# Gated linear attention with all chunks scored against each other, and RWKV's projections of a half taken for both groups in the order k, r, v

## The chip, the cores and the metric

The kernel runs on one core of one Trainium2 chip. The metric is the device time of one execution in microseconds (us), the median of the runs; lower is better.

## The reference

x is (1, 256, 1024) in float32. A first block (a recurrent layer, a gated feed-forward layer, an attention layer, another feed-forward layer) is followed by a second block of two layers. Each of these two layers projects the normed input and runs three branches on it, a latent attention, an RWKV-7 recurrence and a gated linear attention (GLA), whose gated sum goes through one more projection. The change touches the last two branches. GLA has 4 heads with keys of 128 and values of 256, and the 256 frames are taken as 4 chunks of 64:

```python
cum = jnp.cumsum(log_a.reshape(b, nc, CHUNK, GLA_HEADS, GLA_DK), axis=2)
cum_last = cum[:, :, -1:]
q_dec = q * jnp.exp(cum)
k_inv = k * jnp.exp(-cum)
k_to_end = k * jnp.exp(cum_last - cum)
attn = jnp.einsum('bnihd,bnjhd->bnhij', q_dec, k_inv)
attn = jnp.where(jnp.tril(jnp.ones((CHUNK, CHUNK), bool)), attn, 0.0)
o_intra = jnp.einsum('bnhij,bnjhv->bnihv', attn, v)

def step(state, inp):
    q_c, k_c, v_c, d_c = inp
    o_c = jnp.einsum('bihd,bhdv->bihv', q_c, state)
    state = state * d_c[..., None] + jnp.einsum('bjhd,bjhv->bhdv', k_c, v_c)
    return state, o_c
```

RWKV has 16 heads of 64. Of its streams r, k and v, each shifted by one frame and mixed, the part that matters here is the norm of each head of k and the sum over r, k and r_k:

```python
kk = heads(k * k_k)
kk = kk / jnp.maximum(jnp.sqrt(jnp.sum(kk * kk, axis=-1, keepdims=True)), 1e-12)
k = k * (1 + (a - 1) * k_a)
...
bonus = jnp.sum(r_h * k_h * r_k.astype(f32), axis=-1, keepdims=True) * v_h
```

## The kernel before

All activations stay on the chip; what is streamed from memory is the weights. Every projection goes through `linear` (L303, output with features on the partitions) or `linear_tm` (L328, output with frames on the partitions). Both take a weight block with `weights` (L287): SP starts a DMA into one of four `raw` buffers, ACT casts it to a rounded upper part `hi` (L284), DVE subtracts to get the lower part `lo` (L285), and each product is three matmuls on the PE, hi by hi, hi by lo and lo by hi (L322 to L324 with 256 columns, L350 to L352 with 512). Small products that aren't projections are plain fp32 matmuls; the profile counts each of those twice (an instruction x4 shows as x8).

The program is written out as one stream, and a list scheduler, which counts with modelled times, sets the order of the instructions on each engine before the run. On the chip each engine takes its own list strictly in order and waits at semaphores. The PE's list is mostly projections, with the small products of the three branches put in between them.

The second block's layer `second` (L1022) runs, for each layer, the latent attention, RWKV in two halves (`rwkv`, L1453, hf = 0 and 1, 8 heads each) and GLA (`gla`, L1287). What follows a half of RWKV (inverse and chain) is given out in steps between the projections of the other branches.

One half of RWKV has two groups (g = 0 and 1, four heads each). For each group `rwkv_tiles` (L1478) does in turn: the two low-rank products for decay and gate (`pw`, `pa`, L1506 and L1507), their tanh and exponentials on ACT (L1511 to L1528) with a scan on DVE (L1516), the projection k, squares of k (`rkk`, L1536), the sums of squares over each head by a product with 2 columns (L1541), the root on POOL (`rsqrt`, `root`, L370 to L374, into `rri`), a copy on ACT that spreads it over each head (`rrw`, L1545), four 128x128 products that turn it (L1551), DVE's work on k, the projection r, DVE's products of r and k (L1566), 2-column products for the bonus (L1571), and the projection v. Then `rwkv_products` (L1575) makes the 16 score products of the group (L1585). So each half runs k0, r0, v0, products 0, k1, r1, v1, products 1.

GLA takes two heads at a time (q = 0 and 1). Decays relative to each chunk's own start sit in `ep` (for q), `en` (for k) and `et` (k to the end of its chunk), each 128x2x256. Per head: two transposes of `et` (L1369) and an ACT copy (`ket`), two 128x128 score products (L1375), a mask (`gat`, L1377) that keeps only the two 64x64 blocks on the diagonal, and then a chain over the four chunks: scores by v (L1391, 64x64; L1385 for the second pair of chunks at once), decayed q by the state (L1393), and the next state's addition (`pS`, L1396), which DVE or ACT makes into the state `gS`. One step's L1393 needs the state of the step before.

## Time and profile before

| | before |
|---|---|
| runs, us | 1886.73, 1888.77, 1895.27 (median 1888.77) |
| profiled execution, us | 1890.57, of which the span of the profile is 1888.8 |
| PE busy | 1817.2 us, 96% of the span |
| PE weight loads busy | 1517.8 us, 80% |
| DVE, ACT, POOL busy | 1287.9, 1037.9 and 114.9 us |
| mean granted clock of TensorE | 0.977 of full speed |
| read from memory | 291.58 MB, 156 GB/s over the span |

The profile is of one execution. Its own time, 1890.57 us, is 1.8 us above its span. "Busy" of the PE counts the modelled length of each matmul, and two neighbours overlap in it, so that the time from one start to the next is shorter than the length shown. An idle time stands in square brackets behind the instruction that came after it, with the engine and line whose end released it. The granted clock is a share of full speed: 1.00 is the level of 2.4 GHz and 0.50 that of 1.2 GHz.

### The profile page before, as it was taken

To read this page: it belongs to the slowest core of one execution; us is meant where nothing else is said; L and a number is where in the kernel's file an instruction comes from. 1 tells how busy PE (TensorE), PEld (TensorE's weight loads), DVE (VectorE), ACT (ScalarE), POOL (GpSimd) and SP (SyncE) were. 2 spreads that over 40 slices of the span, in tenths; PEclk is the share of its full clock that TensorE was granted. 3 is DMA by queue.
4 is the path that set the end of the run, shared out by engine and by line. 5 is a ranking of instruction groups with operands and counts; after the bars stand their busy time and mean duration, and the time that the engine had idled before them with its cause. 6 is when DMAs were issued, how large, how long until landed. Compare 5 with 4: busy or idle time off the path is not lost.

```text
span 1888.8 us, 31680 instructions
## 1 busy us (share of the span) xinstructions
PE 1817.2 (96%) x11984; PEld 1517.8 (80%) x11984; DVE 1287.9 (68%) x2824; ACT 1037.9 (55%) x2137; POOL 114.9 (6%) x255
## 2 busy tenths in 40 slices
PE   7999999999989998999999899997999999899997
PEld 6988778877668886998789877796998789877796
DVE  6988788757658874777557754575778566754575
ACT  6786645446544444765566544454665566534453
POOL 0000000002000000020001000100020001000100
PEclk9999999999999999999999899998999999899999
DMA  5534687755247775455244443354455334444263
GB/s 204 179 102 138 219 268 245 239 180 166 91 137 269 260 226 171 144 165 158 90 129 135 134 123 112 102 184 145 135 163 160 99 118 146 127 120 123 90 182 109
DMA packets 108873, 296.79 MB, mean 157 GB/s; under 512 B 34832, under 2 KB 36240, under 8 KB 108592
## 3 DMA queue, kind: packets, MB, share of 16 engines
q1 hardware_dynamic: 106496, 291.54, 48.9%
q10 hardware_dynamic: 2224, 3.22, 0.6%
q8 instruction: 94, 1.54, 0.3%
q14 instruction: 59, 0.48, 0.1%
HBM read 291.58 MB, written 3.15 MB: 156 GB/s over the span
## 4 chain that ended last, share of the span: by engine, by line
PE 53%; DVE 2%; DMA 2%; ACT 2%; POOL 1%; issue 0%; SPq 0%; DVEq 0%; POOLq 0%; ACTq 0%
PE pm L350 7%; PE pm L352 7%; PE pm L351 7%; PE pm L322 6%; PE pm L324 6%; PE pm L323 6%; PE pk L1585 2%; DMA dz<-rZ 1%; PE pS L1396 1%; PE ps L1257 1%; PE ps L1256 1%; DMA Gm<-dz 1%; PE po L1393 1%; PE pk L1692 1%; PE pk L1717 1%; PE po L1391 1%
## 5 line engine op out<-in xcount | busy, mean ns | idle before, releaser
L285 DVE TENSOR_TENSOR lo<-raw,hi 128x512 fp32r<-128x512 f32 (+1 forms) x954 | 645.4, 702 | 285.9 <-ACT hi L284 282.8
L284 ACT CAST hi<-raw 128x512 fp32r<-128x512 f32 (+1 forms) x954 | 559.8, 632 | 483.3 <-PE pm L352 286.7
L322 PE MATMUL pm<-xh,hi 128*128 128x256 f32 (+1 forms) x1224 | 349.0, 287 | 1.1 <-ACT xh L419 1.1
L323 PE MATMUL pm<-xl,hi 128*128 128x256 f32 (+1 forms) x1224 | 349.0, 286 | 0.4 <-DVE xl L420 0.4
L324 PE MATMUL pm<-xh,lo 128*128 128x256 f32 (+1 forms) x1224 | 349.2, 286 | 0.0
L351 PE MATMUL pm<-lo,xh 128*128 128x512 f32 (+1 forms) x832 | 327.9, 397 | 3.2 <-DVE lo L285 3.2
L352 PE MATMUL pm<-hi,xl 128*128 128x512 f32 (+1 forms) x832 | 325.0, 396 | 0.0
L350 PE MATMUL pm<-hi,xh 128*128 128x512 f32 (+1 forms) x832 | 320.2, 398 | 0.6 <-ACT qk L830 0.6
L322 PEld LDWEIGHTS pm<-xh,hi 128*128 128x128 f32 (+1 forms) x1224 | 232.7, 191 | 8.4 <-issue 4.3
L324 PEld LDWEIGHTS pm<-xh,lo 128*128 128x128 f32 (+1 forms) x1224 | 233.2, 191 | 6.2 <-issue 4.9
L323 PEld LDWEIGHTS pm<-xl,hi 128*128 128x128 f32 (+1 forms) x1224 | 233.5, 191 | 4.8 <-issue 2.5
L351 PEld LDWEIGHTS pm<-lo,xh 128*128 128x128 f32 x832 | 156.7, 188 | 40.8 <-DVE lo L285 6.2
L350 PEld LDWEIGHTS pm<-hi,xh 128*128 128x128 f32 x832 | 156.3, 188 | 35.6 <-issue 1.3
L352 PEld LDWEIGHTS pm<-hi,xl 128*128 128x128 f32 x832 | 156.5, 188 | 34.9 <-issue 2.2
L977 DVE SCALAR_TENSOR_TENSOR mda<-mdw,cact,mda 128x256 f32<-128x256 f32 x168 | 80.4, 479 | 5.9 <-DMA mdw<-in_w_ada_dram 4.2
L370 POOL TENSOR_TENSOR rs_y<-rs_m,mhalf 128x8 f32<-128x8 f32 (+3 forms) x30 | 46.9, 1562 | 610.2 <-DVE rs_m L361 553.6
L350 PE MATMUL pm<-hi,oh 128*128 128x512 f32 x192 | 77.2, 405 | 1.8 <-DVE merged L1155 1.8
L351 PE MATMUL pm<-lo,oh 128*128 128x512 f32 x192 | 76.9, 400 | 0.0
L352 PE MATMUL pm<-hi,ol 128*128 128x512 f32 x192 | 75.8, 400 | 0.0
L351 PE MATMUL pm<-lo,ah 128*128 128x512 f32 x176 | 69.5, 397 | 0.0
L352 PE MATMUL pm<-hi,al 128*128 128x512 f32 x176 | 69.3, 396 | 0.0
L350 PE MATMUL pm<-hi,ah 128*128 128x512 f32 x176 | 65.8, 398 | 0.0
(514 smaller groups left out, 2704.5 us busy)
## 6 DMA issues: line engine op xcount, KB each, us to landing
raw<-in_w_gu_dram SPq DMA_DIRECT2D x88, 512.0 KB, 4.6
mdw<-in_w_ada_dram SPq DMA_DIRECT2D x48, 512.0 KB, 5.3
raw<-in_w_dn_dram SPq DMA_DIRECT2D x44, 512.0 KB, 4.0
raw<-in_w_rout_dram SPq DMA_DIRECT2D x16, 512.0 KB, 3.7
raw<-in_w_qk_dram SPq DMA_DIRECT2D x16, 512.0 KB, 3.7
raw<-in_w_k_dram SPq DMA_DIRECT2D x16, 512.0 KB, 4.0
raw<-in_w_r_dram SPq DMA_DIRECT2D x16, 512.0 KB, 4.1
raw<-in_w_v_dram SPq DMA_DIRECT2D x16, 512.0 KB, 3.6
```

What stands on the lines that cost most here:

```text
L284: self.nc.scalar.copy(hi, src)
L285: self.nc.vector.tensor_tensor(lo, src, hi, op=ALU.subtract)
L322: nc.tensor.matmul(o, lhsT=H, rhs=xh[:, kt, :], start=kt == 0 and i == 0, stop=False)
L323: nc.tensor.matmul(o, lhsT=H, rhs=xl[:, kt, :], start=False, stop=False)
L324: nc.tensor.matmul(o, lhsT=L, rhs=xh[:, kt, :], start=False, stop=kt == KT - 1 and i == len(tiles) - 1)
L350: nc.tensor.matmul(ps[g][j], lhsT=xh[:, kt, ts], rhs=hi[:, k, :], start=kt == 0, stop=False)
L351: nc.tensor.matmul(ps[g][j], lhsT=xh[:, kt, ts], rhs=lo[:, k, :], start=False, stop=False)
L352: nc.tensor.matmul(ps[g][j], lhsT=xl[:, kt, ts], rhs=hi[:, k, :], start=False, stop=kt == KT - 1)
L370: nc.gpsimd.tensor_tensor(y, m, self.mhalf[:p].to_broadcast([p, n]), op=ALU.pow)
L977: nc.vector.scalar_tensor_tensor(acc, raw[:, k, :], c, acc, op0=ALU.mult, op1=ALU.add)
L1256: nc.tensor.matmul(ps[:, o], lhsT=qn[:, i, q], rhs=kn[:, i, k], start=True, stop=False)
L1585: nc.tensor.matmul(ps[p][:, c * 128:(c + 1) * 128], lhsT=BK[rows, m, c, :], rhs=AR[rows, m, c, :], start=True, stop=True)
```

## The change

**GLA has no state any more.** The decays are made relative to chunk borders such that every pair of chunks can be scored directly. `ep` has 320 columns: chunks 0 to 2 as before, then chunk 3 relative to the start of chunk 2, then chunk 3 as before. `et` holds the keys of chunks 0 and 1 relative to the start of chunk 2, and those of chunks 0 and 2 to the end of their own chunk. Per head there are then four 64x64 score products and two with 128 columns into 64 rows (the pairs of chunks 0, 1 and 2, 3), one 128x128 product (chunks 2 and 3 against 0 and 1), a causal mask over 128 frames, an ACT copy of the third block, and three full products with v of 256 columns. The transposes, `ket`, `pS`, `gS`, `dcol` and the chain are gone.

**RWKV's tile stage does both groups of a half at once**, in the order decay 0, k0, decay 1, k1, one root for all 16 columns, the spreading and DVE's work for both groups, r0, r1, v0, v1, and then both groups' score products. The weights are asked for in that order, so SP's list has k1 ahead of r0 and both r ahead of v.

```diff
-    c.add("amask", ((i[:, None] <= i[None, :]) & (i[:, None] // 64 == i[None, :] // 64)).astype(f))
+    c.add("amask", (i[:, None] <= i[None, :]).astype(f))
...
-                                       "C": {16: 8, "sm_sc ket gat": (384, 3), "sm_pt go_ gt": (512, 2), "mo gsq": (512, 1)}}, 3, {"C": 2, "A": 3})
+                                       "C": {16: 8, "sm_sc gat": (384, 3), "sm_pt go_ gt": (512, 2), "mo gsq": (512, 1)}}, 3, {"C": 2, "A": 3})
...
-            dcol = new([128, 4, 4], "gdc", bufs=1)
+            last2 = new([128, 4], "glas2", bufs=1)
...
+                ep, en, et = new([128, 2, S + 64], "gep"), new([128, 2, S], "gen"), new([128, 2, S], "get")
...
-                nc.scalar.activation(dcol[:, hq, :], last[:, hq, :], AF.Exp)
-                nc.scalar.activation(ep, cum, AF.Exp, scale=i16)
+                nc.vector.tensor_tensor(last2[:, hq], last[:, hq, 0], last[:, hq, 1], op=ALU.add)
+                nc.scalar.activation(ep[:, :, 0:192], cum[:, :, 0:192], AF.Exp, scale=i16)
+                nc.scalar.activation(ep[:, :, 256:320], cum[:, :, 192:256], AF.Exp, scale=i16)
                 nc.scalar.activation(en, cum, AF.Exp, scale=-i16)
                 for m in range(2):
-                    for c in range(4):
-                        cs = slice(c * 64, (c + 1) * 64)
-                        nc.scalar.activation(et[:, m, cs], cum[:, m, cs], AF.Exp, scale=-i16, bias=last[:, 2 * q + m, c:c + 1])
+                    h = 2 * q + m
+                    nc.scalar.activation(ep[:, m, 192:256], cum[:, m, 192:256], AF.Exp, scale=i16, bias=last[:, h, 2:3])
+                    for at, c, b in ((0, 0, last2[:, h:h + 1]), (1, 1, last[:, h, 1:2]), (2, 0, last[:, h, 0:1]), (3, 2, last[:, h, 2:3])):
+                        nc.scalar.activation(et[:, m, at * 64:(at + 1) * 64], c4[:, m, c, :], AF.Exp, scale=-i16, bias=b)
...
-                    nc.vector.scalar_tensor_tensor(ep, ep, 128 ** -0.5, ps, op0=ALU.mult, op1=ALU.mult)
+                    a, b = ep[:, :, 0:192], ep[:, :, 192:320].rearrange("p m (r s) -> p m r s", s=64)
+                    nc.vector.scalar_tensor_tensor(a, a, 128 ** -0.5, ps[:, :, 0:192], op0=ALU.mult, op1=ALU.mult)
+                    for m in range(2):
+                        nc.vector.scalar_tensor_tensor(b[:, m], b[:, m], 128 ** -0.5, ps[:, m, 192:256].unsqueeze(1).to_broadcast([128, 2, 64]), op0=ALU.mult, op1=ALU.mult)
...
-                    nc.vector.tensor_tensor(et, et, ps, op=ALU.mult)
+                    a, b = et[:, :, 0:128], et[:, :, 128:256].rearrange("p m (r s) -> p m r s", s=64)
+                    nc.vector.tensor_tensor(b, b, ps.rearrange("p m (a b s) -> p m a b s", b=2, s=64)[:, :, :, 0, :], op=ALU.mult)
+                    nc.vector.tensor_tensor(a, a, ps[:, :, 0:128], op=ALU.mult)
...
-                    pt = self.small("ps")
-                    for j in range(2):
-                        nc.tensor.transpose(pt[:, j * 128:(j + 1) * 128], et[:, i, j * 128:(j + 1) * 128], idn)
-                    ket = self.tmp([128, 2, 128], "ket")
-                    nc.scalar.copy(ket, pt[:, 0:256].rearrange("p (j s) -> p j s", s=128))
                     pa = self.small("ps")
                     for j in range(2):
-                        ts = slice(j * 128, (j + 1) * 128)
-                        nc.tensor.matmul(pa[:, ts], lhsT=en[:, i, ts], rhs=ep[:, i, ts], start=True, stop=True)
-                    at = self.tmp([128, 2, 128], "gat")
-                    nc.vector.tensor_tensor(at, pa[:, 0:256].rearrange("p (j s) -> p j s", s=128), am.unsqueeze(1).to_broadcast([128, 2, 128]), op=ALU.mult)
+                        e0, e1, both = ep[:, i, 128 * j:128 * j + 64], ep[:, i, 192 * j + 64:192 * j + 128], ep[:, i, 0:128]
+                        o = pa[:, j * 128:(j + 1) * 128]
+                        oc = o[64:128, :]
+                        if j:
+                            both, oc = ep[:, i, 64:320].rearrange("p (a b s) -> p a b s", b=2, s=64)[:, :, 1, :], oc.rearrange("p (a s) -> p a s", s=64)
+                        nc.tensor.matmul(o[0:64, 0:64], lhsT=en[:, i, 128 * j:128 * j + 64], rhs=e0, start=True, stop=True)
+                        nc.tensor.matmul(o[0:64, 64:128], lhsT=et[:, i, 128 + 64 * j:192 + 64 * j], rhs=e1, start=True, stop=True)
+                        nc.tensor.matmul(oc, lhsT=en[:, i, 128 * j + 64:128 * j + 128], rhs=both, start=True, stop=True)
+                    nc.tensor.matmul(pa[:, 256:384], lhsT=et[:, i, 0:128], rhs=ep[:, i, 128:256], start=True, stop=True)
+                    at = self.tmp([128, 3, 128], "gat")
+                    nc.vector.tensor_tensor(at[:, 0:2, :], pa[:, 0:256].rearrange("p (j s) -> p j s", s=128), am.unsqueeze(1).to_broadcast([128, 2, 128]), op=ALU.mult)
+                    nc.scalar.copy(at[:, 2, :], pa[:, 256:384])
                     po = self.small("po")
                     st, rs = self.tmp([128, 2], "gst"), self.tmp([128, 2], "grs")
                     o = self.tmp([128, 2, 256], "go_")
-                    S_ = None
-                    for j in range(2):
-                        oj = po[:, j * 256:(j + 1) * 256]
-                        if j:
-                            nc.tensor.matmul(oj, lhsT=at[:, j, :], rhs=v[:, j, hv], start=True, stop=False)
-                        for e in range(2):
-                            c = 2 * j + e
-                            rows = slice(64 * e, 64 * e + 64)
-                            cs = slice(c * 64, (c + 1) * 64)
-                            if not j:
-                                nc.tensor.matmul(oj[rows, :], lhsT=at[rows, j, rows], rhs=v[rows, j, hv], start=True, stop=not c)
-                            if c:
-                                nc.tensor.matmul(oj[rows, :], lhsT=ep[:, i, cs], rhs=S_, start=False, stop=True)
-                            if c < 3:
-                                pS = self.small("pS")
-                                nc.tensor.matmul(pS[:, 0:256], lhsT=ket[rows, j, :], rhs=v[rows, j, hv], start=True, stop=True)
-                                new_S = new([128, 256], "gS")
-                                if c:
-                                    nc.vector.scalar_tensor_tensor(new_S, S_, dcol[:, h, c:c + 1], pS[:, 0:256], op0=ALU.mult, op1=ALU.add)
-                                else:
-                                    nc.scalar.copy(new_S, pS[:, 0:256])
-                                S_ = new_S
+                    nc.tensor.matmul(po[:, 0:256], lhsT=at[:, 0, :], rhs=v[:, 0, hv], start=True, stop=True)
+                    nc.tensor.matmul(po[:, 256:512], lhsT=at[:, 2, :], rhs=v[:, 0, hv], start=True, stop=False)
+                    nc.tensor.matmul(po[:, 256:512], lhsT=at[:, 1, :], rhs=v[:, 1, hv], start=False, stop=True)
...
+            self.rwkv_tiles(n, hf, AR, BK, vb, pc, bon, lora, lambda shape, name: r1.tile(shape, F32, name=name))
             for g in range(2):
-                self.rwkv_tiles(n, hf, g, AR, BK, vb, pc, bon, lora, lambda shape, name: r1.tile(shape, F32, name=name))
                 self.rwkv_products(g, AR, BK, Gm)
...
-    def rwkv_tiles(self, n, hf, g, AR, BK, vb, pc, bon, lora, new):
+    def rwkv_tiles(self, n, hf, AR, BK, vb, pc, bon, lora, new):
...
+        def decay(g):
...
+        def project(w, g, evac):
+            self.linear(A["w_" + w + n], hh, hl, evac, groups=[2 * hf + g])
...
         pn = self.small()
+        for g in G:
...
+            decay(g)
+            project("k", g, evac_k)
+            kk[g] = new([128, 2, S], "rkk")
+            for i in range(2):
+                nc.scalar.activation(kk[g][:, i, :], k2[g][:, i, :], AF.Square, scale=self.col("rwkv_k_k" + n, m0 + i))
+            for i in range(2):
+                for j in range(2):
+                    o = (g * 4 + j * 2 + i) * 2
+                    nc.tensor.matmul(pn[:, o:o + 2], lhsT=kk[g][:, i, j * 128:(j + 1) * 128], rhs=heads, start=True, stop=True)
+        ri = self.tmp([128, 16], "rri")
+        self.rsqrt(ri, pn[:, 0:16], 1.0, 1e-24, "8", op1=ALU.max)
+        for g in G:
+            rw[g] = self.tmp([128, 8, 64], "rrw")
+            nc.scalar.copy(rw[g], ri[:, 8 * g:8 * g + 8].unsqueeze(2).to_broadcast([128, 8, 64]))
+            r = rw[g].rearrange("p q c -> p (q c)")
+            pb = self.small()
+            for i in range(2):
+                for j in range(2):
+                    o = (j * 2 + i) * 128
+                    nc.tensor.matmul(pb[:, i * S + j * 128:i * S + (j + 1) * 128], lhsT=r[:, o:o + 128], rhs=idn, start=True, stop=True)
...
+            project("r", g, evac_r)
...
+                    nc.tensor.matmul(pr[:, o:o + 2], lhsT=r2[g][:, i, j * 128:(j + 1) * 128], rhs=heads, start=True, stop=True)
+        nc.scalar.copy(bon, pr[:, 0:16].rearrange("p (j q) -> p j q", j=2))
...
+            project("v", g, evac_v)
```

The program has the same projections as before. How the scheduler lays them out changes in the second block only; three places follow, in rows of the engines' lists. First the PE in half 1 of the first layer, from the sums of squares of the second group (`rkk`) to the score products (`AR`, `BK`). `rrw` is the spread root, `r_...` is the tile of r times k, `cst_all` is a table of constants (identity or head columns), `wa,lora` are the low-rank products. Before:

```order
L1541 MATMUL pk<-cst_all,rkk 128x2 x4
L323 MATMUL pm<-xl,hi 128x256
...
L324 MATMUL pm<-xh,lo 128x256
L1551 MATMUL pk<-cst_all,rrw 128x128 x4
L1571 MATMUL pk<-cst_all,r_10679 128x2 x4
L1585 MATMUL pk<-AR,BK 128x128 x16
L322 MATMUL pm<-xh,hi 128x256
```

With the change:

```order
L1534 MATMUL pk<-cst_all,rkk 128x2 x4
L1490 MATMUL pa<-wa,lora 128x256 x2
L1534 MATMUL pk<-cst_all,rkk 128x2 x4
...
L1545 MATMUL pk<-cst_all,rrw 128x128 x8
L323 MATMUL pm<-xl,hi 128x256
...
L1572 MATMUL pk<-cst_all,r_10484 128x2
L322 MATMUL pm<-xh,hi 128x256
L1572 MATMUL pk<-cst_all,r_10484 128x2 x3
...
L1572 MATMUL pk<-cst_all,r_10561 128x2 x3
```

The root product, the bonus products and the score products stood next to each other, with 26 projection matmuls between L1541 and L1551 and none after it. Now 44 projection matmuls and two low-rank products stand between the last L1534 and L1545, 84 projection matmuls between L1545 and the first L1572, and the score products come later, in pieces between projections. From the first low-rank product to L1545 the list has 65 projection matmuls, four pairs of low-rank products and eight 2-column products.

Second, ACT in the same place, from the first tanh of the decays (`ld`) to the copy `rrw`. Before:

```order
L1511 ACTIVATE ld<-pa,hcols_7424 128x256 x2
...
L1512 ACTIVATE aa<-pa,hcols_7424 128x256 x2
L1450 ACTIVATE k_10574<-pm,mu_7429 128x256
L1536 ACTIVATE rkk<-k_10574,pv 128x256
L1528 ACTIVATE rf<-aa,hcols_7424 128x256
L1520 ACTIVATE rpp<-rcum 128x8x64
L1522 ACTIVATE rpi<-rcum 128x512
L1528 ACTIVATE rf<-aa,hcols_7424 128x256
L284 CAST hi<-raw 128x512 x2
L1536 ACTIVATE rkk<-k_10574,pv 128x256
L1545 COPY rrw<-rri 128x512
```

With the change:

```order
L1511 ACTIVATE rf<-aa,hcols_7424 128x256 x2
L1503 ACTIVATE rpp<-rcum 128x8x64
L1505 ACTIVATE rpi<-rcum 128x512
L1495 ACTIVATE ld<-pa,hcols_7424 128x256 x2
L1497 ACTIVATE ld<-ld 128x512
L1503 ACTIVATE rpp<-rcum 128x8x64
L1505 ACTIVATE rpi<-rcum 128x512
L1496 ACTIVATE aa<-pa,hcols_7424 128x256 x2
L284 CAST hi<-raw 128x512 x2
L1511 ACTIVATE rf<-aa,hcols_7424 128x256
L1539 COPY rrw<-rri 128x512 x2
```

The decays of the second group (`ld`, `rpp`, `rpi`, `aa`) now stand ahead of the copies of the root. The two squares `rkk` and one piece of v have gone from this stretch.

Third, the PE in GLA, one head (`gen`, `gep`, `get` are the tiles `en`, `ep`, `et`; between the rows shown stand projections). Before:

```order
L1369 MATMUL ps<-cst_all,get 128x128 x2
L1375 MATMUL ps<-gep,gen 128x128 x2
...
L1391 MATMUL po<-gv,gat 64x256
L1396 MATMUL pS<-gv,ket 128x256
L1391 MATMUL po<-gv,gat 64x256
...
L1393 MATMUL po<-gS,gep 64x256
L1396 MATMUL pS<-gv,ket 128x256
L1385 MATMUL po<-gv,gat 128x256
```

With the change:

```order
L1383 MATMUL ps<-gep,gen 64x64
L1384 MATMUL ps<-gep,get 64x64
L1385 MATMUL ps<-gep,gen 64x128
L1383 MATMUL ps<-gep,gen 64x64
L1384 MATMUL ps<-gep,get 64x64
L1385 MATMUL ps<-gep,gen 64x128
L1386 MATMUL ps<-gep,get 128x128
...
L1393 MATMUL po<-gv,gat 128x256
...
L1394 MATMUL po<-gv,gat 128x256
L1395 MATMUL po<-gv,gat 128x256
```

Before, two more L1393 and one more L1396 of the head follow further down, each a state later. Now all scores of a head stand together, and the three products with v follow some 20 projection matmuls later, with nothing after them that depends on a state.

## Rows read from the trace of the kernel before

**Rows 1.** The profile's page: busy time, share of the span and instructions.

```profile
PE 1817.2 (96%) x11984; PEld 1517.8 (80%) x11984; DVE 1287.9 (68%) x2824; ACT 1037.9 (55%) x2137; POOL 114.9 (6%) x255
```

**Rows 2.** Waits of PE: line, released by: us in total, times, longest us.

```profile
PE pk L1571 <- DVE r L1566: 6.6, 2, 3.3
...
PE pk L1551 <- ACT rrw L1545: 4.1, 2, 2.0
...
PE pk L1692 <- ACT SAV L1685: 2.8, 2, 1.4
...
PE po L1391 <- DVE gat L1377: 1.4, 2, 1.1
```

**Rows 3.** PE by line: busy us, mean ns, then idle before.

```profile
L1396 PE MATMUL pS<-gv,ket 64*128 64x256 f32 x48 | 17.2, 440 | 0.0
L1393 PE MATMUL po<-gS,gep 128*64 128x256 f32 x48 | 15.5, 404 | 0.0
L1692 PE MATMUL pk<-SAV,BKt 128*64 128x64 f32 x192 | 12.3, 244 | 2.8 <-ACT SAV L1685 2.8
L1391 PE MATMUL po<-gv,gat 64*64 64x256 f32 x32 | 11.2, 434 | 1.4 <-DVE gat L1377 1.4
...
L1385 PE MATMUL po<-gv,gat 128*128 128x256 f32 x16 | 5.6, 431 | 0.0
...
L1375 PE MATMUL ps<-gep,gen 128*128 128x128 f32 x32 | 5.1, 280 | 0.0
...
L1369 PE MATMUL ps<-cst_all,get 128*128 128x128 f32 x16 | 3.7, 272 | 0.0
```

**Rows 4.** PE's timeline in GLA: start us, length us, instruction.

```profile
1089.09 0.64 PE L1391 MATMUL po<-gv,gat 64*64 64x256 f32 x2
1089.67 0.70 PE L1396 MATMUL pS<-gv,ket 64*128 64x256 f32 x2
1090.29 0.64 PE L1391 MATMUL po<-gv,gat 64*64 64x256 f32 x2
1090.86 0.39 PE L323 MATMUL pm<-xl,hi 128*128 128x256 f32 x1
```

**Rows 5.** Windows, both GLAs: stretch, length, busy by engine, PEclk, DMA share, GB/s.

```profile
1085.00:1203.00 118.00, 116.25 (x909) 87.91 (x908) 60.40 (x134) 50.57 (x112) 9.16 (x25) 0.97 0.36 108
1655.00:1775.00 120.00, 117.56 (x938) 88.30 (x937) 59.48 (x131) 50.67 (x114) 9.16 (x25) 0.96 0.36 105
```

**Rows 6.** PE's timeline, first layer, half 1, second group.

```profile
1044.12 0.28 PE L323 MATMUL pm<-xl,hi 128*128 128x256 f32 x1
1044.24 0.28 PE L324 MATMUL pm<-xh,lo 128*128 128x256 f32 x1
...
1050.99 1.87 PE L1571 MATMUL pk<-cst_all,r 128*128 128x2 f32 x8 [3.29 <-DVE r L1566]
```

**Rows 7.** Windows behind these waits, first and second layer; columns as in rows 5.

```profile
1050.99:1062.55 11.56, 11.56 (x62) 11.32 (x63) 4.62 (x10) 9.85 (x30) 0.00 (x0) 0.50 0.17 27
1620.63:1629.16 8.53, 8.53 (x48) 8.29 (x49) 3.93 (x9) 8.30 (x26) 0.00 (x0) 0.50 0.11 16
```

**Rows 8.** PE's timeline, first layer, half 1, first group.

```profile
1004.31 1.13 PE L1506 MATMUL pa<-wa,lora 64*128 64x256 f32 x4
...
1018.11 1.05 PE L1551 MATMUL pk<-cst_all,rrw 128*128 128x128 f32 x8
```

**Rows 9.** ACT's timeline, same place.

```profile
1007.38 0.84 ACT L1511 ACTIVATE ld<-pa,hcols 128x256 f32<-128x256 f32 x2
...
1012.34 0.66 ACT L1520 ACTIVATE rpp<-rcum 128x512 f32<-128x512 f32 x1
...
1015.43 0.62 ACT L1545 COPY rrw<-rri 128x512 f32<-128x512 f32 x1
```

**Rows 10.** DVE's timeline, same place.

```profile
1010.37 1.26 DVE L1516 TENSOR_TENSOR_SCAN rcum<-cst_sb,ld 128x256 f32<-128x256 f32 x2
```

**Rows 11.** POOL by line and form: the root over 16 columns.

```profile
L370 POOL TENSOR_TENSOR rs_y<-rs_m,mhalf 128x16 f32<-128x16 f32 x4 | 11.6, 2895 | 74.9 <-DVE rs_m L361 42.4 <-DVE sm_st L910 32.5
```

More of the change, by code (lines that the diff above doesn't have):

```diff
@@ L1309, in gla @@
                 cum = self.tmp([128, 2, S], "gcum")
-                ep, en, et = new([128, 2, S], "gep"), new([128, 2, S], "gen"), new([128, 2, S], "get")
+                ep, en, et = new([128, 2, S + 64], "gep"), new([128, 2, S], "gen"), new([128, 2, S], "get")
                 ps = pss[q]
@@ new lines, in rwkv_tiles, with evac_r @@
+        pr = self.small()
+        for g in G:
+            m0 = 4 * hf + 2 * g
+            def evac_r(_, ps):
+                r2[g] = new([128, 2, S], "r2")
+                self.shifted(n, ps, [r2[g][:, i, :] for i in range(2)], m0)
+            project("r", g, evac_r)
+            nc.vector.tensor_tensor(AR[:, ms[g], :, 64:128], c4(r2[g]), pp[g][:, :, :, 1:], op=ALU.mult)
+            for i in range(2):
+                nc.vector.scalar_tensor_tensor(r2[g][:, i, :], r2[g][:, i, :], self.col("rwkv_r_k" + n, m0 + i), k2[g][:, i, :], op0=ALU.mult, op1=ALU.mult)
+            for j in range(2):
+                for i in range(2):
+                    o = (j * 4 + 2 * g + i) * 2
+                    nc.tensor.matmul(pr[:, o:o + 2], lhsT=r2[g][:, i, j * 128:(j + 1) * 128], rhs=heads, start=True, stop=True)
@@ L1575, in rwkv_products, with evac_v @@
+        nc.scalar.copy(bon, pr[:, 0:16].rearrange("p (j q) -> p j q", j=2))
+        for g in G:
+            def evac_v(_, ps):
+                self.shifted(n, ps, [vb[:, 2 * g + i, 64:] for i in range(2)], 16 + 4 * hf + 2 * g)
+            project("v", g, evac_v)
     def rwkv_products(self, g, AR, BK, Gm):
```

125 lines of the change are left out of this document (45 added, 80 removed).

## The prediction

> **What bounds the kernel now.** I read the page first. PE is busy for 1817.2 of 1888.8 us [rows 1], so time is won where PE does less, waits less, or runs at a higher clock, and other engines matter only where PE waits for them. The list of PE's waits comes second: four lines of it touch the change, 6.6 us at L1571, 4.1 at L1551, 2.8 at L1692 and 1.4 at L1391, each twice, once per layer [rows 2]. Third is PE by line, which prices what GLA does now [rows 3]; fourth the timeline and the windows by granted clock around those places [rows 4 to 7], where the reader is to see that a wait may cost more than its length: behind the longest one the clock stands at 0.50, the 1.2 GHz level, for 11.56 and 8.53 us. Last are the queues ahead of the root copy, where the new order could make a new wait [rows 8 to 11].
>
> **A. GLA's products (26 us).** Eight heads in all (four per layer). Removed are the lines L1369, L1375, L1385, L1391, L1393 and L1396, together 3.7 + 5.1 + 5.6 + 11.2 + 15.5 + 17.2 = 58.3 us busy [rows 3]. Added per head: three products with 256 columns, two with 128 columns into 64 rows and one into 128, four with 64 columns. A 256-column product costs 5.6/8 = 0.70 us (an instruction is two records), a 128-column one 5.1/16 = 0.32, one with 64 columns 12.3/96 = 0.128 by L1692 [rows 3]. So 24 x 0.70 + 24 x 0.32 + 32 x 0.128 = 16.8 + 7.7 + 4.1 = 28.6, and 29.7 go. L1692's shape is not that of the new ones; if 64 columns cost as much as 128, the added work is 34.7 and 23.6 go. Busy counts overlaps: L1391, L1396, L1391 are 0.64 + 0.70 + 0.64 = 1.98 us busy and take 1.77 from the first start to the next instruction [rows 4], so I take 0.9 of it, 26.7 to 21.2. I choose 26, near the price by columns, since L1391 and L1385 cost alike for 256 columns (0.70) whatever their rows, which says that columns set the price; ends 21 and 29.7.
>
> The three small products of rows 4 run one after another, although two of them use different quarters of the array. The Trainium skill ("TensorEngine Tiling (Array Packing)", Tiling Modes, Key Properties) says that different tiles can work in parallel; by it half of L1391 would hide, A would be 26 - 0.9 x 5.6 = 21 and the time 1841. The trace's 1.77 us against 1.98 disagrees.
>
> DVE loses 16 state updates and gains a few short operations, ACT loses copies and gains some exponentials of 64 columns. Both are busy for about half of GLA's stretches (60.4 and 50.6 of 118 us [rows 5]), so I cost this at nothing. If that cover were gone PE would wait at the mask, L1391's place, which now costs 1.4 us.
>
> **B. GLA's waits (4 us).** L1391's 1.4 and L1692's 2.8 us [rows 2] stand in these stretches, where three or four small products in a row found nothing else to do. In the new list the products with v come some 20 projection matmuls (of 0.12 us with 256 columns [rows 6], longer with 512) after the scores, and no state has to come back. Ends 0 and 4.2.
>
> **C. The clock in GLA (6 us).** The granted clock is 0.97 over 118 us and 0.96 over 120 [rows 5], which loses 0.03 x 118 + 0.04 x 120 = 8.3 us against 1.00. I take most of it as a consequence of the gaps and thin products there; ends 0 and 8.3.
>
> **D. The waits of half 1 (7.5 us).** Second group, each layer: L1551 waits for the root copy (4.1 in two) and L1571 for r (6.6), 10.7 us [rows 2]. They arise because these products come last, with only 26 projection matmuls behind the squares. Now 44 projection matmuls and two low-rank products stand between the squares and L1545: 44 x 0.12 + 1.13 = 6.4 us, and 84 more, 10.1 us, before the first L1572 [rows 6, 8]. The old distance from L1551's start to L1571's is 1050.99 - (1044.24 + 0.28 + 2.0) = 4.5 us for one group [rows 2, 6], so at most 9 for two: covered. One root over 16 columns takes 2.9 us in its longest step [rows 11], plus short ones, and fits in the 6.4.
>
> What is late next is ACT's queue ahead of the root copy. Before, the first tanh starts 3.07 us after the first low-rank product, and the copy ends at 1016.05, 8.67 us later, while PE needs it at 1018.11: 2 us to spare [rows 8, 9]. The change puts two pairs of half-width steps (0.84 each) and three full-width ones (0.66 each) ahead of the copy, 3.7 us, and takes out net two half-width ones (0.84). The second group's exponentials also wait for the second scan, 1.26 us [rows 10]. The copy so ends 3.07 + 8.67 + 2.8 + 1.26 = 15.8 us after the first low-rank product. PE gets there after 65 x 0.12 + 4 x 1.13 + 1.9 = 14.2 us (the eight 2-column products as L1571's 1.87 us for four at half clock [rows 6]). That leaves a wait of 1.6 us per layer at L1545, so D is 10.7 - 3.2 = 7.5; ends 0 and 10.7. Half 0 had no such wait, and its list is spread in the same way: nothing.
>
> On SP the weight requests of k1, r and v trade places and stay as many; on POOL there are four roots fewer, which shortens nothing that ends last; ACT's bonus copies become one per half. Nothing for these: the DMA engines are at 0.11 to 0.17 of their time behind half 1's waits [rows 7] and at 0.36 in GLA [rows 5].
>
> **E. The clock behind these waits (9 us).** 11.56 and 8.53 us at 0.50 [rows 7] would take half at 1.00: 10.0. Waits of 1.6 us in place of 2.0 and 3.3 close together should not bring the fall back; I keep 1 us for it. Ends 0 and 10.
>
> **Sum.** 26 + 4 + 6 + 7.5 + 9 = 52.5 us. The profiled execution took 1890.57, so it would take 1838.1. The median of the runs, 1888.77, lies 1.8 below it: **1836 us**, 2.8% less.
>
> **The rivals.**
> *The clock stays low* (0.19). Nothing shows that GLA's falls come from gaps: its longest waits are 1.1 and 1.4 us [rows 2], and only those of half 1, 2.0 and 3.3, have a fall right behind them [rows 6, 7]. Then C is lost and, the cause being in the thin products, half of E: 1836 + 6 + 4.5 = 1847. The Trainium skill ("TensorE: Matmul & The Clock Gate", Why this matters for your kernels) warns of idle gaps only from a length that GLA's do not reach; by that C would stay lost.
> *Small tiles do run in parallel* (0.04): the 1841 above. Rows 4 speak against it.
> *The wait moves to the root copy* (0.12). ACT's queue turns out some 4 us longer than counted, PE waits over 5 us per layer at L1545, and the clock falls as before. D and E are lost: 1836 + 16.5 = 1853. For it: the queue is within 1.6 us of PE by my count, and ACT was busy without a break there. Against: only short steps were added.
> *The freed time becomes waits* (0.06). PE in GLA catches up with its weights or with RWKV's chain, and half 1 stalls as before; A, B, D and E are lost: 1836 + 46.5 = 1883, no change that can be told. Against: DVE and ACT stand at half there [rows 5].
> *Slower* (0.05). ACT's queue in the tile stage holds PE in all four halves, since both groups' decays now stand ahead of any root. To end 0.5% above 1888.8, at 1898.2, it must cost 62 us over the forecast, 15.5 per half; from there it decides. With 16 per half the time is 1836 + 64 = 1900. That asks for a queue of some 30 us instead of 15.8, which no row supports.
>
> **How the numbers follow.** The forecast has 0.54. A measurement of this kernel can tell 0.5%, 9.4 us, from no change. Faster are the forecast and the first three rivals, 0.54 + 0.19 + 0.04 + 0.12 = 0.89; I give 0.88 and the rest to no change, 0.07; slower 0.05. With all terms at their upper ends (29.7 + 4.2 + 8.3 + 10.7 + 10.0 = 62.9) the time is 1825.9, and the runs go 2 us below their median: low end 1823. The high end is the third rival with A at 21 and C lost, 1853 + 5 + 6 = 1864. What is outside are the last two rivals and a little below, under 0.2.
>
> **What the profile of the changed kernel would show.** A: no L1391 to L1396 of a state; the new lines L1383 to L1386 and L1393 to L1395 sum to 28 to 35 us busy. B, C: no waits over 1 us in GLA, clock 0.99 or more there. D: L1545 waits some 1 to 2 us twice, L1572 nothing. E: no stretch at 0.50 behind half 1. PE busy about 1770 to 1785 us. I am wrong if PE's waits at L1545 exceed 4 us each, if the clock in GLA stays at 0.97, or if the new products cost over 40 us.

## The result, and the profile after

The changed kernel takes 1838.64 us (median of 4 runs, 1835.16 to 1840.54); before, run beside it, takes 1887.75 us. The ratio is 0.9727, with a 95% interval of 0.9705 to 0.975. The forecast was 1836, from 1823 to 1864. The profiled execution went from 1890.57 to 1839.51 us, its span by 51.1 us, from 1888.8 to 1837.7. The page of the changed kernel, busy time by engine, against [rows 1]:

```profile
span 1837.7 us, 31584 instructions
...
PE 1786.2 (97%) x11952; PEld 1507.0 (82%) x11952; DVE 1280.9 (70%) x2820; ACT 1038.1 (56%) x2133; POOL 105.8 (6%) x235
```

PE is busy for 31.0 us less, and the other 20.1 us were time in which it stood. PE's waits in the changed kernel, longest first (line, released by: us in total, times, longest):

```profile
PE pk L404 <- DVE xn L456: 27.3, 3, 11.7
PE po L404 <- DVE xl L420: 4.4, 1, 4.4
PE pm L351 <- DVE lo L285: 1.9, 5, 0.6
PE pm L322 <- ACT xh L419: 1.5, 1, 1.5
```

None of the four waits of [rows 2] has a successor anywhere in this list: the changed lines L1545, L1572, L1393 and L1698 wait for nothing. So 6.6 + 4.1 + 2.8 + 1.4 = 14.9 us of standing are gone, and with them some smaller waits of the second block (2.0 us for DVE's `z` in the inverse, 1.8 us for `merged` at the last projection).

The windows of the changed kernel (columns as in [rows 5]): both GLAs, then the stretches behind the squares of half 1, first and second layer.

```profile
1079.00:1195.00 116.00, 116.00 (x957) 96.32 (x956) 69.23 (x150) 60.06 (x127) 10.19 (x25) 1.00 0.48 146
1630.00:1745.00 115.00, 115.00 (x962) 95.35 (x960) 67.08 (x135) 59.44 (x127) 10.47 (x25) 1.00 0.47 141
1006.13:1016.37 10.24, 10.24 (x42) 9.18 (x42) 4.43 (x10) 8.18 (x17) 4.43 (x7) 0.50 0.24 76
1548.85:1559.09 10.24, 10.24 (x42) 9.18 (x42) 4.51 (x10) 8.21 (x17) 4.43 (x7) 0.50 0.21 73
```

In GLA the clock is 1.00 and PE never stands, where it was 0.97 and 0.96 [rows 5]. But half 1 of RWKV still has 10.24 us at 0.50 in each layer, like the stretches of [rows 7], although PE is busy in it without a break. The timeline of PE around the first of them shows where it begins:

```profile
1002.76 1.13 PE L1491 MATMUL pa<-wa,lora 64*128 64x256 f32 x4
1003.82 0.38 PE L322 MATMUL pm<-xh,hi 128*128 128x256 f32 x1
1004.04 0.28 PE L323 MATMUL pm<-xl,hi 128*128 128x256 f32 x1
1004.16 0.95 PE L1534 MATMUL pk<-cst_all,rkk 128*128 128x2 f32 x8
1005.04 1.13 PE L1490 MATMUL pa<-wa,lora 64*128 64x256 f32 x4
1006.10 1.87 PE L1534 MATMUL pk<-cst_all,rkk 128*128 128x2 f32 x8
1007.82 0.56 PE L324 MATMUL pm<-xh,lo 128*128 128x256 f32 x1
...
1018.13 1.95 PE L1545 MATMUL pk<-cst_all,rrw 128*128 128x128 f32 x16
```

The first four norm products (x8) take 0.95 us, the next four 1.87. Between 1002.76 and 1006.10 PE did almost only low-rank and 2-column products, and no square bracket shows a wait.

GLA's new products by line (busy us, mean ns of one), which answer to [rows 3]:

```profile
L1385 PE MATMUL ps<-gep,gen 128*64 128x128 f32 x32 | 5.5, 295 | 0.0
L1393 PE MATMUL po<-gv,gat 128*128 128x256 f32 x16 | 5.2, 404 | 0.0
L1395 PE MATMUL po<-gv,gat 128*128 128x256 f32 x16 | 4.8, 379 | 0.0
L1394 PE MATMUL po<-gv,gat 128*128 128x256 f32 x16 | 4.7, 378 | 0.0
L1383 PE MATMUL ps<-gep,gen 128*64 128x64 f32 x32 | 4.6, 234 | 0.0
L1384 PE MATMUL ps<-gep,get 128*64 128x64 f32 x32 | 4.2, 225 | 0.0
L1386 PE MATMUL ps<-gep,get 128*128 128x128 f32 x16 | 3.9, 326 | 0.0
```

They sum to 32.9 us busy, inside the 28 to 35 that were forecast. Yet busy tells little here. In the timeline of one head two instructions at a time start within some 10 ns of each other:

```profile
1079.29 0.27 PE L1383 MATMUL ps<-gep,gen 128*64 128x64 f32 x1
1079.30 0.32 PE L1385 MATMUL ps<-gep,gen 128*64 128x128 f32 x1
...
1079.45 0.22 PE L1384 MATMUL ps<-gep,get 128*64 128x64 f32 x1
1079.46 0.27 PE L1385 MATMUL ps<-gep,gen 128*64 128x128 f32 x1
...
1079.94 0.49 PE L1386 MATMUL ps<-gep,get 128*128 128x128 f32 x2
```

The six products into 64 rows of PSUM take 0.65 us from 1079.29 to 1079.94. Two that write different halves of the rows run side by side.

To place the 51.1 us I added up, line by line over the whole trace, the time from each PE instruction's start to the next one's start, or to its own end if PE stood after it. The column of lost clock is half of that time where the granted clock was 0.50. Over all lines, those without a row of their own included, the times sum to PE's busy time on the page.

| PE, start to start, us | before | lost clock | after | lost clock |
|---|---|---|---|---|
| GLA's products (L1369 to L1396; L1383 to L1395) | 49.5 | 1.7 | 17.5 | 0.0 |
| low-rank products (L1506, L1507; L1490, L1491) | 10.6 | 0.0 | 16.7 | 2.0 |
| norm, root and bonus products | 21.9 | 1.8 | 21.2 | 1.7 |
| score products (L1585; L1591) | 28.5 | 5.1 | 26.8 | 0.0 |
| RWKV's chain | 74.3 | 2.0 | 71.2 | 0.0 |
| projections | 1446.8 | 13.0 | 1448.3 | 13.6 |
| all of PE | 1817.2 | 30.8 | 1786.2 | 22.9 |

GLA's products alone account for 32.0 of the 51.1 us, and the low-rank products give 6.1 back, 2.0 of them by the clock. The score products give something back too, which the row hides: without the lost clock they went from 23.4 to 26.8 us, 3.4 more.

### The profile page after: what moved, and what is told of

It reads as the page before. It is cut to its first block, busy times and chain, and to the rows that moved or that the text cites. A ratio compares the mean times of both kernels' runs of the same rounds, so it can differ in the third digit from the quotient of the medians.

```text
span 1837.7 us, 31584 instructions
## 1 busy us (share of the span) xinstructions
PE 1786.2 (97%) x11952; PEld 1507.0 (82%) x11952; DVE 1280.9 (70%) x2820; ACT 1038.1 (56%) x2133; POOL 105.8 (6%) x235
## 4 chain that ended last, share of the span: by engine, by line
PE 93%; DMA 2%; DVE 2%; ACT 1%; issue 1%; POOL 0%; SPq 0%; DVEq 0%; POOLq 0%; ACTq 0%
PE pm L351 16%; PE pm L350 16%; PE pm L352 16%; PE pm L322 9%; PE pm L324 9%; PE pm L323 9%; PE pk L1591 1%; DMA mdw<-in_w_ada_dram 1%; PE ps L1257 1%; PE ps L1256 1%; PE pk L404 1%; DVE lo L285 1%; PE pp L917 1%; PE pk L1723 1%; PE pk L1690 1%; PE pk L1698 1%
## 5 line engine op out<-in xcount | busy, mean ns | idle before, releaser
L370 POOL TENSOR_TENSOR rs_y<-rs_m,mhalf 128x16 f32<-128x16 f32 (+3 forms) x26 | 45.8, 1763 | 661.2 <-DVE rs_m L361 628.7
```

Of the source, the lines that this page charges most:

```text
L370: nc.gpsimd.tensor_tensor(y, m, self.mhalf[:p].to_broadcast([p, n]), op=ALU.pow)
```

## The experiments

All times are medians. The kernel before was run again beside each group of kernels, on the same chip: 1890.55 us beside the first four below, 1888.86 beside the next four, 1889.46 beside the last three.

**The two parts apart.** The first kernel has only the edits in GLA, the mask and the temporary rings, the second only those in `rwkv` and `rwkv_tiles`.

```diff
-    c.add("amask", ((i[:, None] <= i[None, :]) & (i[:, None] // 64 == i[None, :] // 64)).astype(f))
+    c.add("amask", (i[:, None] <= i[None, :]).astype(f))
...
```

> The kernel before with the GLA part of the change alone. Theory (GLA carries the gain): the small products of GLA take some 50 us of PE's time from start to start before and 17.5 after, its two waits 4.2 us and the clock falls in its stretches 8.5 us; all three go, so about 1888 - 42 = 1846 us, with the waits and the stretch at half clock in RWKV's half 1 as before. Rival (as forecast, RWKV's part is worth 16.5 us): 1888 - 36 = 1852 us. If the falls of the clock in GLA stay, 1855.

Measured: 1856.16 us (1852.04 to 1858.75), ratio 0.9819 (0.9784 to 0.9853), 34.4 us less. That is 4 us above the rival's number and next to the 1855 us for falls of the clock that stay in GLA; but they did not stay, its GLA window stands at 1.00. What is missing went elsewhere. A new wait shows, for ACT's `gv`, which the list of before doesn't have. Waits of PE, and the windows of GLA in the first layer and behind half 1 in both:

```profile
PE pk L1564 <- DVE r L1559: 6.6, 2, 3.3
PE pm L322 <- ACT gv L1343: 6.4, 2, 3.2
```

```profile
1084.00:1190.00 106.00, 105.69 (x865) 87.25 (x864) 63.10 (x140) 54.63 (x117) 9.60 (x25) 1.00 0.48 141
1049.52:1066.59 17.07, 11.88 (x63) 11.57 (x64) 6.93 (x17) 11.22 (x34) 0.00 (x0) 0.50 0.33 77
1599.06:1616.13 17.07, 10.66 (x57) 10.35 (x58) 8.01 (x18) 11.22 (x34) 0.00 (x0) 0.50 0.38 95
```

ACT comes late to GLA's `gv` copies behind half 1, 6.4 us. The stretch at 0.50 is 17.07 us long there in each layer; PE works in it for 11.88 and 10.66 us, half of which is lost, 11.3 us against 10.0 before [rows 7]. Together that is 7.7 us, about what is missing between 34.4 and the theory's 42.

```diff
+            self.rwkv_tiles(n, hf, AR, BK, vb, pc, bon, lora, lambda shape, name: r1.tile(shape, F32, name=name))
             for g in range(2):
-                self.rwkv_tiles(n, hf, g, AR, BK, vb, pc, bon, lora, lambda shape, name: r1.tile(shape, F32, name=name))
                 self.rwkv_products(g, AR, BK, Gm)
...
```

> The kernel before with RWKV's new order alone. Theory: the waits of half 1 go (10.7 us), a stretch at half clock of some 10 us stays in each layer, and the low-rank and score products cost some 7 us more, so 1888 - 8 = 1880 us. Rival (as forecast, waits and clock together): 1888 - 16.5 = 1871 us.

Measured: 1871.08 us (1865.75 to 1874.9), ratio 0.9894 (0.9863 to 0.9926), 19.5 us less. That is the rival's number, but not its mechanism. Its windows, half 1 and then GLA:

```profile
1007.06:1017.30 10.24, 10.24 (x41) 8.68 (x40) 4.65 (x9) 8.08 (x18) 4.42 (x7) 0.50 0.24 75
1570.26:1577.09 6.83, 6.83 (x27) 5.77 (x27) 3.45 (x7) 5.46 (x13) 4.98 (x7) 0.50 0.13 39
1076.00:1198.00 122.00, 120.00 (x951) 91.60 (x952) 66.30 (x145) 53.49 (x119) 10.41 (x25) 0.99 0.39 119
1640.00:1760.00 120.00, 118.25 (x972) 90.58 (x970) 63.77 (x138) 53.78 (x119) 10.25 (x25) 0.99 0.38 114
```

The stretches at 0.50 stay in half 1, as the theory said. What came on top of the waits of half 1 are other small waits and two of the four falls of the clock in GLA. In the trace of before each of these four begins at the end of a wait of PE among small products or within 2 us behind it: two at L1391's waits for `gat` (0.37 and 1.05 us), two at L1692's for `SAV` (1.39 and 1.38 us). One of them in PE's timeline of before; L1391 takes 1.11 us in place of the 0.64 of [rows 4]:

```profile
1683.82 1.11 PE L1391 MATMUL po<-gv,gat 64*64 64x256 f32 x2 [1.05 <-DVE gat L1377]
```

With RWKV's part alone the waits for `gat` are gone and their falls with them; the waits for `SAV` stay, 2.8 us in all, and so do their falls.

The parts add up: 34.4 + 19.5 = 53.9, beside the 49.1 to 55.2 us that the whole change won in its two measurements. But they do not add up piece by piece: two of GLA's falls went in either part, and the wait for `gv` stands in the first part alone.

**Why the clock falls without a wait.** The norm products of both groups are issued together behind both projections k; nothing else changes.

```diff
+        for g in G:
             for i in range(2):
                 for j in range(2):
                     o = (g * 4 + j * 2 + i) * 2
                     nc.tensor.matmul(pn[:, o:o + 2], lhsT=kk[g][:, i, j * 128:(j + 1) * 128], rhs=heads, start=True, stop=True)
```

On PE's list in half 1 all low-rank products now come first, then 12 projection matmuls, then the eight norm products, then 66 projection matmuls.

> The changed kernel with the 2-column products of the norms of both groups issued together behind k1, so that on PE in half 1 projections stand between them and the low-rank products. Theory (the clock falls in half 1 because the low-rank and 2-column products stand nearly in a row there, with no wait at all): the granted clock stays at 1.00 there, twice 5 us are won, 1828 us. Rival (the fall belongs to what comes before, or to any order of both groups at once): still two stretches at 0.50 of some 10 us, 1838 us.

Measured: 1828.0 us (1827.41 to 1829.38), ratio 0.967 (0.9645 to 0.9694), as the theory said. The windows of half 1 of both layers, from the low-rank products to the root's:

```profile
999.20:1018.00 18.80, 18.80 (x136) 16.84 (x136) 11.33 (x20) 17.33 (x37) 6.02 (x8) 1.00 0.32 101
1536.50:1555.30 18.80, 18.80 (x137) 16.79 (x136) 11.27 (x20) 17.29 (x37) 6.02 (x8) 1.00 0.32 99
```

The same products, spread differently, leave the clock at 1.00. Next, the norm products stay where they are but have 64 columns:

```diff
-                    o = (g * 4 + j * 2 + i) * 2
-                    nc.tensor.matmul(pn[:, o:o + 2], lhsT=kk[g][:, i, j * 128:(j + 1) * 128], rhs=heads, start=True, stop=True)
+                    o = (g * 4 + j * 2 + i) * 64
+                    nc.tensor.matmul(pn[:, o:o + 64], lhsT=kk[g][:, i, j * 128:(j + 1) * 128], rhs=self.const("heads64"), start=True, stop=True)
...
```

The lines left out move the head columns to the front of their table, so that 64 columns can be read from it, and let the root's first step on DVE pick the two useful columns of each product.

> The changed kernel with the norm products of 64 columns in place of 2, in the same place and order; only two columns of each are used. Theory (the 2-column products are what lowers the clock): no stretch at 0.50 in half 1, 1828 us. Rival (it is any run of small products that stand together, or the low-rank ones): the two stretches stay, 1838 us or a little above.

Measured: 1828.95 us (1828.61 to 1829.36), ratio 0.9674 (0.9649 to 0.9698); the granted clock is 1.00 in both halves 1:

```profile
1001.00:1018.50 17.50, 17.50 (x126) 15.51 (x125) 11.28 (x20) 17.39 (x36) 5.67 (x8) 1.00 0.34 106
1543.00:1561.00 18.00, 18.00 (x149) 17.48 (x148) 14.58 (x27) 13.09 (x28) 5.06 (x7) 1.00 0.38 121
```

In the first layer the norm products stand where they stood, but the list behind them is not quite the same: 63 instead of 37 projection matmuls follow the last low-rank product before L1545's successor. The fall began ahead of that place in the changed kernel. In the second layer the scheduler also moved some of the norm products away from the low-rank ones, so only the first layer shows the width alone.

One execution says little here, because the changed order does not fall each time. It stands in both layers of four profiled executions (the changed kernel twice, RWKV's part alone, and the version with two roots below); the clock fell in six of these eight places. With the norm products together or wide it fell in none of four, and all eight runs of these two kernels end between 1827.4 and 1829.4 us. So the 2-column products between low-rank ones are what the clock answers to here, and wider ones in their place cost no time of PE that shows. Whether the low-rank products are needed for the fall as well is not shown.

The same edit in the kernel before, for norm and bonus products:

> The kernel before with the norm and bonus products of 64 columns in place of 2, in the same place and order; only two columns of each are used. Theory (in the kernel before the clock falls because of the waits of 2.0 and 3.3 us themselves): waits and the stretches at 0.50 stay, 1887 to 1892 us. Rival (there too it is the 2-column products): the stretches go, some 10 us less, 1880 us.

Measured: 1890.83 us, ratio 1.0009 (0.9995 to 1.0023): no change. PE's timeline and the window behind:

```profile
1047.02 1.16 PE L1555 MATMUL pk<-cst_all,rrw 128*128 128x128 f32 x8 [2.03 <-ACT rrw L1549]
1051.46 1.75 PE L1575 MATMUL pk<-cst_all,r 128*128 128x64 f32 x7 [3.29 <-DVE r L1570]
```

```profile
1048.90:1062.50 13.60, 11.04 (x59) 10.70 (x60) 7.16 (x15) 10.31 (x30) 0.00 (x0) 0.50 0.26 69
```

Waits and stretch stay. The clock there drops at 1048.9, inside the wait of 3.29 us, before any bonus product. So there are two ways into the same loss: standing, in the kernel before, and thin work without standing, in the changed one. The first is read from where the fall begins; no run takes the wait away and leaves the small products around it as they are.

**What of RWKV's part is needed.** First a root for each group instead of one over 16 columns:

```diff
-        self.rsqrt(ri, pn[:, 0:16], 1.0, 1e-24, "8", op1=ALU.max)
...
+        for g in G:
+            ri[g] = self.tmp([128, 8], "rri")
+            self.rsqrt(ri[g], pn[:, 8 * g:8 * g + 8], 1.0, 1e-24, "8", op1=ALU.max)
...
```

> The changed kernel with a root of its own for each group of a half (8 columns each, one behind the other on POOL) in place of one over 16. Theory (the order of the projections does the work, the shared root adds nothing): the same as the changed kernel, 1836 to 1841 us, no wait at the root's products. Rival (the shared root is part of the gain): the second group's copy comes later, waits of 1 to 2 us per half return, 1843 us or more.

Measured: 1842.22 us (1840.37 to 1844.71), ratio 0.9747 (0.973 to 0.9765). That lies between the two expectations, and the interval overlaps that of the changed kernel (0.9705 to 0.975). Waits of PE:

```profile
PE pm L324 <- DVE lo L285: 5.3, 2, 3.0
...
PE pk L1547 <- ACT rrw L1541: 0.9, 1, 0.9
```

One wait of 0.9 us at the root's products is of the kind that the rival named. The larger part, 5.3 us, is elsewhere: DVE stands for 4.74 us at the first instruction of RWKV's inverse, for a DMA, with weights queued behind it. That came with the shift of the list, so what the shared root is worth by itself stays open, at most the few us between these kernels. In the second layer of this execution the clock held at 1.00 through the low-rank and norm products and fell for 3.41 us further down, where score and bonus products stand in a row, again without a wait.

Then the other way round: GLA's part, the old order k, r, v in each group with two roots, and only the score products moved behind both groups.

```diff
             for g in range(2):
                 self.rwkv_tiles(n, hf, g, AR, BK, vb, pc, bon, lora, lambda shape, name: r1.tile(shape, F32, name=name))
+            for g in range(2):
                 self.rwkv_products(g, AR, BK, Gm)
```

> The kernel before with the GLA part of the change, and of RWKV's part only that the score products of both groups come behind both groups' tiles; projections stay in the order k, r, v for each group, with two roots. Theory (what leaves PE waiting in half 1 is that the last group's root, bonus and score products have no projections between them): some 36 projections now follow the squares and some 50 the root's products, the wait for r goes and about 1 us of the wait for the root stays, so about 1846 us, with a stretch at half clock where 32 score products stand in a row. Rival (the order k, k, r, r, v, v is needed): waits as in the kernel with GLA's part alone, 1856 us.

Measured: 1828.84 us (1825.6 to 1830.8), ratio 0.9674 (0.9656 to 0.9692): better than either expectation and than the changed kernel. No wait at the root or bonus products is left, only 3.2 us for `gv` behind the scores, and the clock stays at 1.00 in both halves 1:

```profile
PE pm L322 <- ACT gv L1343: 3.2, 2, 1.6
```

```profile
1003.00:1055.00 52.00, 50.40 (x383) 46.45 (x383) 38.69 (x74) 40.46 (x95) 8.01 (x12) 1.00 0.43 132
1540.00:1590.00 50.00, 48.40 (x369) 44.57 (x368) 37.64 (x73) 39.53 (x92) 8.01 (x12) 1.00 0.45 138
```

I had expected the 32 score products in a row to bring the clock down; they didn't, though no more than 24 of them stand in a row in this list. The low-rank products take 13.1 us from start to start there, against 16.7 in the changed kernel, and the score products 23.6 against 26.8.

**Neighbours on the array.** In the kernel before, the two 64x64 products of chunks 0 and 1 are put next to each other, ahead of the state product that stood between them.

```diff
+                        else:
+                            for e in range(2):
+                                rows = slice(64 * e, 64 * e + 64)
+                                nc.tensor.matmul(oj[rows, :], lhsT=at[rows, j, rows], rhs=v[rows, j, hv], start=True, stop=not e)
...
-                            if not j:
-                                nc.tensor.matmul(oj[rows, :], lhsT=at[rows, j, rows], rhs=v[rows, j, hv], start=True, stop=not c)
```

> The kernel before with the two 64x64 products of the first pair of chunks next to each other (scores by v of chunks 0 and 1, different quarters of the array) instead of with a state product between them. Theory (neighbours on different parts of the array overlap, and each change of shape costs some 0.1 us): the pair takes 0.5 to 0.7 us where two took 1.2, 8 heads, so 4 to 6 us less than before, about 1884 us. Rival (they run one after another, as the trace of before suggests): 1 us less, 1889 us.

Measured: 1883.0 us (1880.38 to 1885.39), ratio 0.996 (0.9945 to 0.9975), 5.9 us less. PE's timeline, to be read against [rows 4]:

```profile
1090.82 0.65 PE L1389 MATMUL po<-gv,gat 64*64 64x256 f32 x4
1091.40 0.70 PE L1398 MATMUL pS<-gv,ket 64*128 64x256 f32 x2
1092.03 0.39 PE L323 MATMUL pm<-xl,hi 128*128 128x256 f32 x1
```

Both products (x4) now take 0.58 us together, from 1090.82 to 1091.40, as long as one took before. GLA's products come to 43.5 us from start to start; before they took 49.5, of which 1.7 were lost clock, so 4.3 us went by the order alone. The theory holds.

**A version ahead of both.** Two kernels and the changed one, run beside each other on one chip. In the first, both projections v come behind both groups:

```diff
-        self.linear(A["w_v" + n], hh, hl, evac_v, groups=gg)
+        return lambda: self.linear(A["w_v" + n], hh, hl, evac_v, groups=gg)
...
```

> GLA's part of the change, RWKV's tiles in the old order for each group (two roots) but both v projections behind both groups, and the score products behind those. Theory (enough projections between the last group's root and its score products is all that RWKV's part needs): no waits of PE in half 1 over 1 us, no stretch at 0.50 there, the low-rank products of the second group still side by side, 1823 to 1828 us. Rival (32 score products in a row lower the clock or hold the next projection): 1832 us or more.

> The kernel with GLA's part and RWKV's score products last, on the same chip as the changed kernel: 1826 to 1831 us, 8 to 12 us under it. Rival (the difference is one between chips): equal within 3 us.

> The changed kernel itself on the same chip as its neighbours in this call: 1836 to 1841 us, with the two stretches at 0.50 in half 1 of each layer. If it came to 1830 or less, those stretches would be a matter of the single execution and not of the order.

Measured: 1828.61 us with v last (1825.95 to 1828.81); 1826.83 us with the score products last (1824.78 to 1829.19), ratio 0.9667 (0.9648 to 0.9687); 1834.31 us for the changed kernel (1831.35 to 1837.36), ratio 0.9707 (0.9686 to 0.9727). With v last there is no wait over 0.6 us in half 1 and no stretch at 0.50, as the theory said, and the time is 0.6 us above its range; it gains nothing over the simpler version with the score products last. That one is as fast as expected, and 7.5 us under the changed kernel, a little less than the 8 to 12 that were expected, so the difference was not one between chips. PE is busy for 13.8 us less in it (1765.4 against 1779.2 us): 5.8 by the clock, 3.2 at the score products, 1.7 at the low-rank products and the rest spread over other lines. Its waits are 4.2 us longer.

The changed kernel came out 2 us below what I had expected of it. Its profiled execution here had the stretch at 0.50 in the first layer only. Windows of half 1 in both layers, and the timeline of the second layer:

```profile
1003.27:1013.51 10.24, 10.24 (x42) 9.17 (x42) 4.44 (x10) 8.23 (x17) 4.44 (x7) 0.50 0.27 77
1543.00:1557.00 14.00, 13.18 (x94) 11.52 (x93) 7.89 (x14) 12.63 (x28) 4.99 (x7) 1.00 0.21 61
```

```profile
1555.46 0.71 PE L1545 MATMUL pk<-cst_all,rrw 128*128 128x128 f32 x4 [0.82 <-ACT rrw L1539]
```

Where the clock stayed at 1.00, PE came to L1545 before the root copy and waited 0.82 us. Where it fell, PE was late enough not to wait. So the fall is not certain in every execution of this order, against what I had expected of this run, and it hides the wait that the forecast had counted.

## Why the prediction was right, step by step

The total was right to 3 us, most of the mechanisms were right, some sizes were not, and errors of both signs met in the sum. At an equal clock GLA's products gave 4.3 us more than forecast, the clock in GLA 2.5 more, the waits of half 1 3.2 more, and small waits that I had not counted 5.2. Against that the clock behind half 1 gave 9.2 less, and the low-rank and score products took back 7.5. That the sum came so close is luck in good part.

- **A, 26 us from GLA's products; measured 32.0 from start to start (49.5 to 17.5), 30.3 without the lost clock that C counts.** The right side, the wrong size. I priced by busy time and took "0.9 of it" on both sides; on the chip the old products took 0.85 of their busy time (49.5 of 58.3) and the new ones 0.53 (17.5 of 32.9). I read 1.77 us against 1.98 in [rows 4] as disagreement with the Trainium skill's sentence ("TensorEngine Tiling (Array Packing)", Tiling Modes, Key Properties) that tiles work in parallel. The runs side with the page: neighbours on different parts of the array do overlap, 0.58 us for two, and in rows 4 they were not neighbours, since L1396 stood between them. The rival of 1841 us fails all the same, since in the list of before none of GLA's products stood so that it could overlap; what overlaps are the new ones, which the rival left out.
- **Missed: the low-rank products, 6.1 us dearer, 2.0 of them by the clock.** L1506 and L1507 use two halves of the array and often ran side by side before; in the new list more of L1490 and L1491 are split by projections (from 1002.76 on they run one kind at a time). I had counted their number, not their neighbours. Missed as well: the score products, 3.4 us dearer without the clock.
- **B, 4 us: 4.2.** Right; and 5.2 us more of small waits went that I had not counted (all gaps together fell from 62.0 to 41.9 us, by 20.1, of which B and D are 14.9).
- **C, 6 us: all of the 8.5 that the clock cost in GLA.** Right side, slightly small. The first rival, which lost C, was wrong here. I had no row for the cause; the trace has one, since the four falls begin at or shortly behind waits of 0.37 to 1.39 us. The page of the Trainium skill that stood beside that rival ("TensorE: Matmul & The Clock Gate", Why this matters for your kernels) warns of longer gaps, and here the clock fell behind shorter ones. Not each of them brings a fall: in the kernel before with 64 columns both waits of 1.39 us for `SAV` have none behind them. GLA's edit took away the waits and the thin products around them together, so how much is due to either is not shown.
- **D, 7.5 us: 10.7 in the profiled execution.** The wait of 1.6 us that I kept for the root copy did not show, because PE came late at half clock. At full clock it is there, 0.82 us, half of what I counted.
- **E, 9 us: none of it came.** This is the step that failed: "Waits of 1.6 us in place of 2.0 and 3.3 close together should not bring the fall back". The fall came back with no wait at all. PE had worked at 0.50 for 11.56 and 8.53 us behind the waits of half 1 [rows 7], and now did so for 10.24 and 10.24: 10.0 us lost before, 10.2 after. The whole falls of before were longer, 13.65 and 10.24 us, but the part ahead of rows 7 lies inside the waits that D counts. I had taken waits to be the only cause; norm products of 2 columns between low-rank ones were another: with these products together or with 64 columns PE's lost clock fell from 22.9 us to 12.7 and 12.3. D and E together were forecast at 16.5 and gave 10.5.

Of the rivals, the clock that stays low was half right, in half 1 and not in GLA. The root copy's wait exists and is small. PE's freed time did not turn into other waits, and nothing was slower.

## What to carry to other kernels

Price small matmuls by the time from start to start with their real neighbours: busy time overstates those that overlap, and the order of the list decides whether they can. Removing waits does not by itself keep the clock up: look for runs of thin products too, and spread them between wide ones or widen them; either was enough here. And when a change reorders a stage, try the smallest piece of the reorder alone; here moving only the score products behind both groups, beside GLA's part, did more than the full new order.

## What the runs showed of the hardware

A change of shape on PE costs time: in the trace of before L1391 and L1396, alternating, run 0.58 and 0.63 us from start to start (1089.09, 1089.67, 1090.29 in [rows 4]), while the products of the same 256 columns that follow each other in one shape in the changed kernel, L1394 and L1395, start 0.42 us apart:

```profile
1086.52 0.59 PE L1394 MATMUL po<-gv,gat 128*128 128x256 f32 x2
1086.94 0.59 PE L1395 MATMUL po<-gv,gat 128*128 128x256 f32 x2
```

So GLA's old chain paid some 0.15 to 0.2 us for each of its changes of shape, which no busy time shows as such. That it is the change and not the 64 rows is seen at L1491 in the changed kernel, which has the shape of L1396: the two of them from 1002.76 on take 1.06 us to the next product, 0.53 each against L1396's 0.63: two products share what each L1396 paid alone.

And the granted clock may fall in one execution of a stretch and not in another of the same kernel, as in half 1 of the changed kernel's second layer.
